# One layer of a hybrid decoder: the score matmuls of head pairs, and four waiting times in the order's planner

## The chip, the cores and the metric

The kernel runs as one program on one core of a Trainium2 chip. Its time is the device time of that core in microseconds (us); lower is better. Three runs of the kernel before gave 2163.1, 2163.2 and 2168.06 us, the median is 2163.2 us. One more execution was profiled; all views of the trace come from that one.

Engines are named as in the profile: PE is TensorE's matmuls and PEld its weight loads, DVE is VectorE, ACT is ScalarE, POOL is GpSimd, SP is SyncE, which issues every DMA of this kernel ("SPq").

## The reference, cut to what matters

```
h = rmsnorm(x);  proj = h @ w_in                        # 2048 prompt rows and 32 sample rows
qa, ka, va, ga, qb, kb, vb, gb, ma, mb = split(proj)
q, k = per-head RMS norm (gain, and 1/8 for q), head_dim 64
branch A: 8 query heads, 2 kv heads, window 128, a learned sink per head
branch B: 3 groups of 8 heads, (window, dilation) = (128,1), (512,4), (2048,16)
   # positions fall into residue classes; a block of 128 queries sees its own block of keys and the one before
   s = q @ k.T ;  s += relative position bias ;  p = exp(s - max) ;  o = p @ v / sum(p)
   # group outputs are merged with weights from max and sum
ya = (o_a * silu(ga)) @ w_up_a ;  yb = (o_b * silu(gb)) @ w_up_b
y = x + (sigmoid(ma) * ya + sigmoid(mb) * yb) @ w_out
```

The sample rows do the same against caches of past keys. New keys (after the norm and gain) and values are outputs too.

## The kernel before

**Precision.** Every large matmul is done in f16 with operands split in two: `hi` is the rounded value, `lo` the rest. A projection is three matmuls per 128 rows of contraction (hi·hi, hi·lo, lo·hi), each with a 128x128 stationary operand from the normalised input `hT` and 512 columns of weights moving. For the scores a head's 64 values of `hi` and 64 of `lo` lie under each other on the 128 partitions, for q and for k. `t.KT[0]` holds k as (hi, lo), and `t.KT[1]` a copy with the halves exchanged, (lo, hi). So two full matmuls per head give all four products: q against `KT[0]` is hi·hi + lo·lo, q against `KT[1]` is hi·lo + lo·hi, summed in the same place of the PSUM bank.

**Stages.** First come the sigmoid gates (to about 400 us). Then branch B's groups 3, 2 and 1 (to about 766, 1113 and 1436 us), each 16 tiles of 128 queries; then branch A, 16 more tiles (to about 1850 us); then up-projections and the output projection. In the 64 tiles of attention, a tile is a chain of projections q, k, v (in A: q, kv and two gates), each into one of five shared PSUM banks, 24 matmuls of 512 columns each, and a process `attend`. 22 of the 64 tiles see one block of keys, 42 see two.

**A tile's keys.** `k_chain` copies the projection out of PSUM (L730), `norm` takes squares, sums, the power of minus a half on POOL and multiplies (L738 to L751), `parts` splits into hi and lo (L303, L308), `k_turn` sends the result through a transposing DMA (L167) into `KT[0]` and then makes `KT[1]` by two DVE copies, L773, of 64 partitions each. The keys of a tile have one such place (two slots, one for even and one for odd tiles), so `k_turn` is told to wait until the tile before has been scored.

**Scores.** `attend` starts a tile's `unit`s: with two blocks of keys four units of two heads (four matmuls of 256 columns), with one block two units of four heads (eight matmuls of 128). Unit after unit takes bank 3 or bank 4 in turn (`bank[3 + y]`, lock `S_l[y]`) and fills its 512 columns. DVE reads the bank (L801: adds the bias, takes the row maximum; one instruction a head, and its accumulator read), ACT takes exponentials (L815), the result is split, transposed by DMA, and multiplied with v into bank 7 (matmuls of 64 columns).

**What sets the order.** Nothing is reordered by a compiler. The kernel is written as processes over a clock of its own (`Clock`): each instruction is appended to its engine's queue when the process reaches it, and the process then sleeps until the planner's estimate of its end (`use`, `move`, `LAT`). The clock advances by the nominal cost of each matmul. So a time in a `yield` decides only how many instructions of other processes are appended ahead, on every engine's queue; the waits between engines are semaphores that are put in by the framework from the tiles and banks that instructions touch. A matmul of a tile's first unit that finds its keys missing holds up everything behind it on PE's queue, projections of other tiles included.

**Helpers.** All matmuls are recorded at L259 and transposes on PE at L263. `load_bias` (L901) fetches the gains and biases of a group at its start. `to_pairs` (L1333) scales a finished output of branch A and transposes it on PE.

Of the kernel before, what the change touches and what calls it, by code (L numbers as in the profile page):

```python
# [150 lines left out]
def hybrid_kernel(ctx, tc, xp, xs, ca, cb1, cb2, cb3, rel_bias, norm_gain, w_in, qga, kga, sinks, qgb, kgb,  # L151
# [245 lines left out]
    def set_scale(b, am):  # L397
# [19 lines left out]
        if b.gained:  # L417
            V.tensor_scalar(b.c, b.pw, 2.0 ** -24, None, op0=OP.mult)
            V.tensor_tensor(b.tmp, b.s, b.s, op=OP.mult)
            V.tensor_scalar(b.epsc, b.tmp, EPS * 2.0 ** 20, None, op0=OP.mult)  # L420
            V.tensor_scalar(b.cu, b.c, 2.0 ** 6, None, op0=OP.mult)
            V.tensor_scalar(b.ch, b.c, 0.5, None, op0=OP.mult)
            V.tensor_scalar(b.vs, b.s, 2.0 ** -10, None, op0=OP.mult)
            yield use("V", 400)
# [256 lines left out]

    QT = [cv(8, P, dt=F16) for _ in range(2)]
    A_K = cv.off
    KTa = [cv(2, 2, P, dt=F16) for _ in range(2)]
# [41 lines left out]
    def norm(src, p0, n, nh, blk, scr, dst, gains=None, raw=None):  # L726
# [14 lines left out]
        V.tensor_scalar(st[:, 1, :nh], st[:, 0, :nh], 1.0 / 64, blk.epsc[p0:p0 + n], op0=OP.mult, op1=OP.add)  # L741
# [12 lines left out]
    def parts(dst, src, nh, scale, perm=False):  # L754

        x = heads(src)
        o = dst[:, :nh * 64].bitcast(F16).rearrange("p (h a d) -> p h a d", a=2, d=64)
        hi, lo = o[:, :, 0], o[:, :, 1]
        if perm:
            x = x.rearrange("p (j u) d -> p u j d", j=2)  # L760
            hi, lo = (v.rearrange("p (u j) d -> p u j d", j=2) for v in (hi, lo))
        yield from split(hi, lo, x, scale, nh * 64)

    def turn(dst, src, nh):

        SP.turn(dst, src[:, :nh * 64].bitcast(F16))
        yield ck.come

    def k_turn(nh, dst, cur):
        x, y = (v[:, :, cur] for v in dst)  # L770
        yield from turn(x, kn, nh)
        for j in range(2):
            V.tensor_copy(y[64 - 64 * j:128 - 64 * j], x[64 * j:64 * j + 64])  # L773
            e = use("V", 33 * nh + 65)
        yield e

    def unit(t, y, n3, us, last):
# [8 lines left out]
        for a, (x, u, j) in enumerate(hs):  # L786
            for p_ in range(2):
                ks = t.KT[p_][:, x if g else j]
                ks = ks.rearrange("p s t -> p (s t)") if nk == 2 else ks[:, cur]
                mm(bank[3 + y][:, a * w:(a + 1) * w], t.QT[:, x], ks, p_ == 0, p_ == 1, cost(w))  # L790
# [4 lines left out]
        for a, (x, u, j) in enumerate(hs):  # L795
            h = t.head(u, j)
            o, i_, b_ = sb[:, a * w:(a + 1) * w], bank[3 + y][:, a * w:(a + 1) * w], bias[:, h, (2 - nk) * P:]
# [11 lines left out]
        S_l[y].put()  # L809
# [91 lines left out]
    def load_bias(g, last):  # L901

        SP.dma_start(GR[:, g % 2], dram(GRd, 64 * g, [[0, P], [1, 64]]))
        SP.dma_start(gk_row[:, g % 2], dram(kga[0] if g == 0 else kgb[0, g - 1], 0, [[0, P], [1, 64]]))

# [51 lines left out]
    def b_tile(g, t, tok, rows, nk, cur, last, par):  # L957
# [25 lines left out]
        def k_chain(b):  # L983
            yield from stK_l.get()
            yield from norm(b.ap[:, :], 0, P, 8, blocks[f"k{g}"], kn, stK, raw=(b.lock, kn_l))
            yield from parts(kn, stK, 8, 2.0 ** 11)
# [52 lines left out]
    KT.append(cv(8, 2, P, dt=F16))  # L1039
# [16 lines left out]
    def sample_proj(g, box):  # L1056
# [20 lines left out]
        def k_chain():  # L1077
            k = sx[32:64, :kw]
            yield from norm(b.ap[32:64, :kw], 32, NS, nh, blocks[names[1]], d["sk"][1], k)
            V.tensor_tensor(heads(k), heads(k), gk_row[32:64, g % 2:g % 2 + 1].to_broadcast([NS, nh, 64]), op=OP.mult)  # L1080
            yield use("V", tv(kw))
            SP.dma_start(Ks[g][:, :], k)
            SP.dma_start(new_s[g][0].rearrange("n t a h d -> (n t) a (h d)")[:, 0], k)
# [249 lines left out]
    def to_pairs(n, o, t0, fcol):  # L1333
# [8 lines left out]
        yield ck.now + 200  # L1342
# [11 lines left out]
    def a_tile(i, t, par):  # L1354
# [52 lines left out]
        def k_chain(b):  # L1407
# [6 lines left out]
            yield from norm(k, 0, P, 2, blocks["kv0"], kn, k)  # L1414
# [4 lines left out]
            yield from parts(kn, k, 2, 2.0 ** 11)  # L1419
# [427 lines left out]
```

## Time and profile before

| | |
|---|---|
| median of three runs | 2163.2 us |
| the profiled execution's own time | 2170.46 us |
| its span, first to last instruction | 2168.6 us |
| PE busy in the span | 2029.2 us, 94% |
| DVE / ACT / POOL busy | 1386.0 / 1053.3 / 707.9 us |
| mean granted TensorE clock | 0.979 |

The profiled execution is 7.3 us above the median of the runs. The busy share of PE is that of matmuls that overlap in their pipeline, so a stretch of PE time is better read from the starts of successive matmuls. A wait of an engine is the idle time just before an instruction, put down to what ended it.

### The profile page before, as it was taken

The numbers are of one execution on the slowest core, as the hardware profiler recorded it, in microseconds if no ns is written. First come the engines' busy times: TensorE is split into PE (matmuls) and PEld (weight loads), VectorE is DVE, ScalarE is ACT, GpSimd is POOL, SyncE is SP. The second block draws the span as 40 slices with busy tenths as digits, with TensorE's granted clock in tenths as the row PEclk, the third lists the DMA queues.
The fourth block names the chain that finished last, engine by engine and source line by source line (L and its number), as shares of the span: only waits on it lengthen the run. The fifth ranks groups of instructions, "written<-read, shape, count | busy, mean of one in ns | idle before, by whom it ended". The sixth has DMA issues, their size and how long they took to land.

```text
span 2168.6 us, 36145 instructions
## 1 busy us (share of the span) xinstructions
PE 2029.2 (94%) x13042; PEld 1135.8 (52%) x13042; DVE 1386.0 (64%) x3305; ACT 1053.3 (49%) x2526; POOL 707.9 (33%) x530
## 2 busy tenths in 40 slices
PE   6999999999999899898999999997899997999999
PEld 3555555666665455554544554544455555444464
DVE  5546662576754577773767885869788898642331
ACT  5432312555555667665776766765456555300000
POOL 1000000255632245541324552426655653220110
PEclk9999999999999999999999999999999998999999
DMA  7896571368879568978857878744434366332322
GB/s 225 175 300 230 203 269 57 115 175 201 217 174 264 139 134 203 215 157 228 218 113 151 168 167 160 172 102 107 79 82 108 96 176 175 110 107 88 115 85 93
DMA packets 528389, 344.34 MB, mean 159 GB/s; under 512 B 397585, under 2 KB 427762, under 8 KB 528210
## 3 DMA queue, kind: packets, MB, share of 16 engines
q1 hardware_dynamic: 528210, 342.04, 61.4%
q8 instruction: 102, 1.67, 0.3%
q14 instruction: 77, 0.63, 0.1%
HBM read 193.53 MB, written 62.43 MB: 118 GB/s over the span
## 4 chain that ended last, share of the span: by engine, by line
PE 59%; DVE 15%; DMA 12%; ACT 5%; issue 4%; SPq 2%; POOL 2%; DVEq 0%; POOLq 0%; ACTq 0%
PE bank L259 58%; DMA arena<-arena 7%; DVE arena L308 3%; DVE arena L773 2%; DMA out_dram<-arena 2%; DVE slot L473 2%; DVE arena L801 2%; ACT arena L815 2%; SPq L161 1%; SPq L167 1%; ACT slot L470 1%; DMA hT<-arena 1%; ACT arena L303 1%; DVE arena L751 1%; POOL nst L743 1%
## 5 line engine op out<-in xcount | busy, mean ns | idle before, releaser
L259 PE MATMUL bank<-slot,hT 128*128 128x512 f16 (+1 forms) x4992 | 1127.6, 377 | 8.0 <-ACT arena L730 4.5
L259 PEld LDWEIGHTS <-hT 128*128 128x128 f16 x4992 | 546.8, 113 | 436.5 <-issue 45.2
L259 PE MATMUL bank<-hT,slot 128*128 128x416 f16 (+4 forms) x2928 | 530.8, 342 | 17.7 <-DVE slot L473 3.8
L743 POOL TENSOR_TENSOR nst<-nst,nhalf 128x8 f32<-128x8 f32 (+2 forms) x136 | 232.4, 1710 | 773.9 <-DVE nst L741 704.6
L259 PEld LDWEIGHTS <-slot 128*128 128x128 f16 x2928 | 287.2, 99 | 251.1 <-DVE slot L473 11.1
L259 PEld LDWEIGHTS <-arena 128*128 128x128 f16 x4336 | 267.9, 99 | 283.1 <-issue 88.9
L259 PE MATMUL bank<-arena 128*128 128x64 f16 (+5 forms) x3746 | 269.9, 230 | 88.6 <-DVE arena L773 44.5
L815 ACT ACTIVATE arena<-arena,ast,inv 128x256 f32<-128x256 f32 (+1 forms) x512 | 283.8, 555 | 7.0
L308 DVE SCALAR_TENSOR_TENSOR arena<-arena 128x512 f16<-128x512 f32 (+1 forms) x292 | 221.6, 772 | 92.2 <-ACT arena L303 91.2
L303 ACT ACTIVATE arena<-arena 128x512 f16<-128x512 f32 (+2 forms) x395 | 231.3, 607 | 98.6 <-DMA arena<-arena 53.8
L1172 POOL TENSOR_TENSOR arena<-arena 128x512 f32<-128x512 f32 (+1 forms) x102 | 140.1, 1373 | 120.7 <-DVE arena L1215 101.4
L259 PE MATMUL bank<-slot,arena 128*128 128x512 f16 x768 | 167.9, 379 | 2.1 <-DVE slot L473 1.6
L473 DVE SCALAR_TENSOR_TENSOR slot<-slot,gsc 128x512 f16<-128x512 f32 (+1 forms) x144 | 107.3, 745 | 86.7 <-ACT slot L470 86.2
L730 ACT ACTIVATE arena<-bank 128x512 f32<-128x512 f32 x112 | 65.8, 589 | 173.4 <-PE bank L259 89.4
L643 ACT ACTIVATE arena<-bank,wst 128x416 f32<-128x416 f32 (+2 forms) x82 | 48.7, 597 | 190.5 <-PE bank L259 162.9
L470 ACT ACTIVATE slot<-slot,gsc 128x512 f16<-128x512 f32 (+1 forms) x144 | 98.1, 681 | 73.2 <-DVE slot L473 63.7
L303 ACT ACTIVATE arena<-arena,yk 128x512 f16<-128x512 f32 (+2 forms) x40 | 25.5, 638 | 201.1 <-POOL arena L1706 186.4
L1706 POOL TENSOR_TENSOR arena<-arena 128x512 f32<-128x512 f32 (+2 forms) x40 | 48.7, 1218 | 221.2 <-DVE arena L1692 201.7
L801 DVE CUSTOM_DVE_ANT_0 arena<-bank,bias 128x128 f32<-128x128 f32 (+1 forms) x296 | 87.4, 343 | 50.2 <-PE bank L259 48.9
L740 DVE TENSOR_REDUCE nst<-arena 128x8 f32<-128x512 f32 (+2 forms) x136 | 85.6, 630 | 42.3 <-ACT arena L738 41.6
L773 DVE COPY arena<-arena 64x1024 f16<-64x1024 f16 (+1 forms) x128 | 77.5, 605 | 54.0 <-DMA arena<-arena 52.3
L810 ACT ACTIVATE ast<-ast,ninv 128x2 f32<-128x2 f32 (+1 forms) x212 | 61.2, 289 | 102.6 <-DVE ast L801 101.7
(167 smaller groups left out, 1758.5 us busy)
## 6 DMA issues: line engine op xcount, KB each, us to landing
arena<-in_cache_b_kv_dram SPq DMA_DIRECT2D x144, 256.0 KB
slot<-in_w_in_dram SPq DMA_DIRECT2D x64, 512.0 KB
arena<-Qs SPq DMA_DIRECT2D x96, 256.0 KB
arena<-in_w_in_dram SPq DMA_DIRECT2D x16, 1024.0 KB
gates<-arena SPq DMA_DIRECT2D x78, 208.0 KB
comb<-arena SPq DMA_DIRECT2D x48, 264.0 KB
arena<-comb SPq DMA_DIRECT2D x48, 264.0 KB
arena<-gates SPq DMA_DIRECT2D x24, 512.0 KB
```

The lines of the kernel that those rows point to most:

```text
L259: T.matmul(out, l, r, start=start, stop=stop)
L303: A.activation(hi, src, AF.Copy, scale=scale)
L308: V.scalar_tensor_tensor(lo, src, scale, hi, op0=OP.mult, op1=OP.subtract)
L470: A.activation(b.part(0, k), src, AF.Copy, scale=sc)
L473: V.scalar_tensor_tensor(b.part(1, k), src, sc, b.part(0, k), op0=OP.mult, op1=OP.subtract)
L730: A.activation(dst, src, AF.Copy)
L740: V.tensor_reduce(st[:, 0, :nh], heads(s), axis=AX.X, op=OP.add)
L743: G.tensor_tensor(st[:, 2, :nh], st[:, 1, :nh], nhalf[p0:p0 + n].to_broadcast([n, nh]), op=OP.pow)
L773: V.tensor_copy(y[64 - 64 * j:128 - 64 * j], x[64 * j:64 * j + 64])
L801: V.tensor_tensor_reduce(out=o, in0=i_, in1=b_, scale=1.0, scalar=-3e38 if g else sinkS[:, u, j:j + 1], op0=OP.add, op1=OP.max, accum_out= ...
L815: A.activation(e, e, AF.Exp, bias=nm[:, x:x + 1], scale=inv[:, g:g + 1], accum_out=l[:, x:x + 1])
L1172: G.tensor_tensor(sprod[:n], q, k, op=OP.mult)
```

## The change

It has two parts.

**The scores.** The layout of q and k within a pair of heads (j = 0, 1) changes: q of head 0 lies as (hi, lo), q of head 1 as (lo, hi); k of head 0 as (lo, hi), k of head 1 as (hi, lo). One full matmul per head now gives the two cross products. `KT[1]` holds only the hi of k, in the 64 partitions where q's hi of that head lies, and a second matmul over these 64 partitions gives hi·hi; lo·lo is no longer computed. The second matmuls of a pair stand in different halves of the array's rows and write to different banks: head 0 to bank 3, head 1 to bank 4. So each unit now writes both banks, and the two units that share them take columns 0 to 255 and 256 to 511 (`place`). The copies behind the turn move half as many values. The factor of 2^11 on k moves from the split into the norm (so that the split has the scale 1.0 and its second step is a plain subtraction), and the gains in `gk_row` are scaled by 2^-11 by one added DVE instruction in `load_bias`, directly behind the DMA that brings them.

**Margins.** Four estimates of the planner grow: behind a turn of q or k by 1500 ns; between the reading of a score bank and its being free for the next unit by 500 ns; in `to_pairs` from 200 to 900 ns.

```
-            V.tensor_scalar(b.ch, b.c, 0.5, None, op0=OP.mult)
+            if b.name[0] == "k":
+                V.tensor_scalar(b.ch, b.epsc, 2.0 ** -22, None, op0=OP.mult)
+            else:
+                V.tensor_scalar(b.ch, b.c, 0.5, None, op0=OP.mult)
...
-    KTa = [cv(2, 2, P, dt=F16) for _ in range(2)]
+    KTa = [cv(2, 2, P, dt=F16), cv(1, 2, P, dt=F16)]
...
-        V.tensor_scalar(st[:, 1, :nh], st[:, 0, :nh], 1.0 / 64, blk.epsc[p0:p0 + n], op0=OP.mult, op1=OP.add)
+        V.tensor_scalar(st[:, 1, :nh], st[:, 0, :nh], 2.0 ** -28 if key else 1.0 / 64, (blk.ch if key else blk.epsc)[p0:p0 + n],
+                        op0=OP.mult, op1=OP.add)
...
-    def parts(dst, src, nh, scale, perm=False):
+    def parts(dst, src, nh, scale, perm=False, key=False):
-        x = heads(src)
-        o = dst[:, :nh * 64].bitcast(F16).rearrange("p (h a d) -> p h a d", a=2, d=64)
-        hi, lo = o[:, :, 0], o[:, :, 1]
-        if perm:
-            x = x.rearrange("p (j u) d -> p u j d", j=2)
-            hi, lo = (v.rearrange("p (u j) d -> p u j d", j=2) for v in (hi, lo))
+        x = heads(src).rearrange("p (j u) d -> p u j d" if perm else "p (u j) d -> p u j d", j=2)
+        o = dst[:, :nh * 64].bitcast(F16)
+        first, then = (bass.AP(tensor=o.tensor, offset=o.offset + c, ap=[o.ap[0], [256, nh // 2], [w, 2], [1, 64]])
+                       for c, w in ((0, 192), (64, 64)))
+        hi, lo = (then, first) if key else (first, then)
         yield from split(hi, lo, x, scale, nh * 64)

     def turn(dst, src, nh):
         SP.turn(dst, src[:, :nh * 64].bitcast(F16))
-        yield ck.come
+        yield ck.come + 1500

     def k_turn(nh, dst, cur):
         x, y = (v[:, :, cur] for v in dst)
         yield from turn(x, kn, nh)
         for j in range(2):
-            V.tensor_copy(y[64 - 64 * j:128 - 64 * j], x[64 * j:64 * j + 64])
-            e = use("V", 33 * nh + 65)
+            V.tensor_copy(y[64 * j:64 * j + 64], x[64 - 64 * j:128 - 64 * j, j::2])
+            e = use("V", 17 * nh + 65)
         yield e

     def unit(t, y, n3, us, last):
...
-        for a, (x, u, j) in enumerate(hs):
-            for p_ in range(2):
-                ks = t.KT[p_][:, x if g else j]
-                ks = ks.rearrange("p s t -> p (s t)") if nk == 2 else ks[:, cur]
-                mm(bank[3 + y][:, a * w:(a + 1) * w], t.QT[:, x], ks, p_ == 0, p_ == 1, cost(w))
+        def place(a, j):
+            o = 256 * y + a // 2 * w
+            return bank[3 + j][:, o:o + w]
+
+        def keys(v):
+            return v.rearrange("p s t -> p (s t)") if nk == 2 else v[:, cur]
+
+        for v in range(0, len(hs), 2):
+            for a, (x, u, j) in enumerate(hs[v:v + 2], v):
+                mm(place(a, j), t.QT[:, x], keys(t.KT[0][:, x if g else j]), True, False, cost(w))
+            for a, (x, u, j) in enumerate(hs[v:v + 2], v):
+                r = slice(64 * j, 64 * j + 64)
+                mm(place(a, j), t.QT[r, x], keys(t.KT[1][r, u if g else 0]), False, True, cost(w) / 2)
...
-            o, i_, b_ = sb[:, a * w:(a + 1) * w], bank[3 + y][:, a * w:(a + 1) * w], bias[:, h, (2 - nk) * P:]
+            o, i_, b_ = sb[:, a * w:(a + 1) * w], place(a, j), bias[:, h, (2 - nk) * P:]
...
-        S_l[y].put()
+        ck.at(ck.now + 500, S_l[y].put)
...
     def load_bias(g, last):
         SP.dma_start(gk_row[:, g % 2], dram(kga[0] if g == 0 else kgb[0, g - 1], 0, [[0, P], [1, 64]]))
+        V.tensor_scalar(gk_row[:, g % 2], gk_row[:, g % 2], 2.0 ** -11, None, op0=OP.mult)
...
-            yield from norm(b.ap[:, :], 0, P, 8, blocks[f"k{g}"], kn, stK, raw=(b.lock, kn_l))
-            yield from parts(kn, stK, 8, 2.0 ** 11)
+            yield from norm(b.ap[:, :], 0, P, 8, blocks[f"k{g}"], kn, stK, raw=(b.lock, kn_l), key=True)
+            yield from parts(kn, stK, 8, 1.0, key=True)
...
     def to_pairs(n, o, t0, fcol):
-        yield ck.now + 200
+        yield ck.now + 900
```

What this makes of the program is seen in the order of instructions. On PE, in the middle of group 1 (its ninth tile, two blocks of keys), the rows of the kernel before are these. `arena` holds q, k and the transposed probabilities, `slot` the weights of the projections, `hT` the normalised input; in brackets stand the semaphores waited for, DMAHW those of DMAs and DVE that of VectorE:

```order
L259 LDWEIGHTS arena_95 [waits DMAHW7_49]
L259 MATMUL bank3_99<-arena_95 128x256 [waits DMAHW4_49]
L259 LDWEIGHTS arena_95
L259 MATMUL bank3_99<-arena_95 128x256 [waits DVE_49]
...
L259 MATMUL bank6_102<-slot0_67,hT0_65 128x512
...
L259 LDWEIGHTS arena_95
L259 MATMUL bank4_100<-arena_95 128x256
```

The tile's first unit fills bank 3 and waits for the turn and for the copies L773; nine projection matmuls later the second unit fills bank 4 and waits for nothing. The same place of the changed program:

```order
L259 LDWEIGHTS arena_95 [waits DMAHW6_49,DMAHW7_49]
L259 MATMUL bank3_99<-arena_95 128x256 [waits DVE_49]
L259 LDWEIGHTS arena_95
L259 MATMUL bank4_100<-arena_95 128x256 [waits DVE_49]
L259 LDWEIGHTS arena_95
L259 MATMUL bank3_99<-arena_95 128x256 [waits DVE_49]
L259 LDWEIGHTS arena_95
L259 MATMUL bank4_100<-arena_95 128x256 [waits DVE_49]
...
L259 MATMUL bank2_98<-slot0_67,hT0_65 128x512
...
L259 MATMUL bank3_99<-arena_95 128x256 [waits DVE_49]
```

Each unit now alternates between the banks, and its first matmul on each bank waits for DVE: the value that it waits for is that of the accumulator read behind the last instruction with which DVE reads this bank for the unit just before, though that one used the other half of the columns. Before, the value was that of the unit before the last. Between the first and the second unit stand six projection matmuls here, where there were nine. Over the program, the first matmul of 156 of the 212 units carries such a wait for the unit directly before it. The number of matmuls is unchanged (12931 in the program), and 512 of the 1024 score matmuls now use 64 rows of the array. Changes of the array's tile shape from one matmul to the next were 76 and are now 581.

In the same program the projections between a tile's k projection and its first score matmul grow: 75 matmuls of 512 columns in the ninth tile of group 3 become 93, 72 in the ninth tile of group 1 become 150.

On DVE, at the start of group 2, the added scaling of the gains stands between work of the running tiles:

```order
L756 TENSOR_TENSOR arena<-arena,nst 128x512
L476 SCALAR_TENSOR_TENSOR slot_68<-slot_68,gsc 128x512
L308 SCALAR_TENSOR_TENSOR arena<-arena 128x512
L919 TENSOR_SCALAR gk_row<-gk_row 128x64
L744 TENSOR_REDUCE nst<-arena 128x8
L745 TENSOR_SCALAR nst<-nst,wst 128x8
```

Row L919 is new, and it waits for the DMA that is issued at the same point of the program.

More of the change, by code (lines that the diff above doesn't have):

```diff
@@ L724, in hybrid_kernel, with norm @@
     start.biased = 4
-    def norm(src, p0, n, nh, blk, scr, dst, gains=None, raw=None):
+    def norm(src, p0, n, nh, blk, scr, dst, gains=None, raw=None, key=False):
         if raw:
@@ L1038, in hybrid_kernel @@
     cv = Carve(sampB["end"])
-    KT.append(cv(8, 2, P, dt=F16))
+    KT.append(cv(4, 2, P, dt=F16))
     QT.append(cv(8, P, dt=F16))
@@ L1079, in k_chain @@
             yield from norm(b.ap[32:64, :kw], 32, NS, nh, blocks[names[1]], d["sk"][1], k)
-            V.tensor_tensor(heads(k), heads(k), gk_row[32:64, g % 2:g % 2 + 1].to_broadcast([NS, nh, 64]), op=OP.mult)
+            V.scalar_tensor_tensor(heads(k), heads(k), 2.0 ** 11, gk_row[32:64, g % 2:g % 2 + 1].to_broadcast([NS, nh, 64]),
+                                   op0=OP.mult, op1=OP.mult)
             yield use("V", tv(kw))
@@ L1413, in k_chain @@
             k = kv[:, :128]
-            yield from norm(k, 0, P, 2, blocks["kv0"], kn, k)
+            yield from norm(k, 0, P, 2, blocks["kv0"], kn, k, key=True)
             if last:
@@ L1418, in k_chain @@
                 SP.dma_start(npa[0, 0].rearrange("t a h d -> t a (h d)")[:, 0], kn[:, 384:])
-            yield from parts(kn, k, 2, 2.0 ** 11)
+            yield from parts(kn, k, 2, 1.0, key=True)
             yield from cond(ck, lambda: prev.scored and (i > 1 or last_b.valued))
```

## The prediction

> **What bounds the kernel now.** I read the page first, then the stages, then PE's waits there.
>
> ```profile
> span 2168.6 us, 36145 instructions
> PEclk9999999999999999999999999999999998999999
> PE 59%; DVE 15%; DMA 12%; ACT 5%; issue 4%; SPq 2%; POOL 2%; DVEq 0%; POOLq 0%; ACTq 0%
> 400.00:766.00 366.00, 340.53 (x2111) 214.62 (x2110) 229.54 (x609) 213.28 (x540) 161.78 (x107) 0.97 0.70 180
> 766.00:1113.00 347.00, 319.73 (x2225) 173.90 (x2224) 239.96 (x584) 230.60 (x574) 133.78 (x89) 0.98 0.81 189
> 1113.00:1436.00 323.00, 308.25 (x2224) 161.03 (x2224) 241.71 (x562) 219.77 (x539) 132.69 (x92) 0.98 0.75 157
> 1436.00:1850.00 414.00, 372.95 (x2829) 224.64 (x2828) 357.05 (x921) 226.89 (x617) 224.53 (x185) 0.96 0.48 117
> ```
>
> The last four rows are group 3, group 2, group 1 and branch A; their columns are the stretch, then busy us of PE, PEld, DVE, ACT and POOL, then granted clock and DMA. PE leads the chain with 59% and is busy in 90 to 95% of these stages, so its work counts almost in full, and so does what it waits for. DVE is next, at 63 to 86%. PE's waits, in these 1450 us:
>
> ```profile
> PE bank L259 <- DVE arena L773: 44.5, 32, 4.7
> PE bank L259 <- DMA arena<-arena: 27.8, 20, 6.5
> PE bank L259 <- DVE ast L801: 12.6, 7, 4.0
> PE bank L263 <- DVE arena L1340: 7.4, 6, 2.4
> PE bank L259 <- ACT arena L730: 4.5, 1, 4.5
> ```
>
> (us in all, times, longest.) The first is the wait of scores for the exchanged keys, the third for a score bank; of the second only 4.2 us stand before scores (3.2 and 1.0 in the rows of the next fence), the rest before the products with v, which the change leaves alone. The clock of 0.96 to 0.98 costs 0.03·366 + 0.02·347 + 0.02·323 + 0.04·414 = 41 us at most.
>
> **PE's work, first what it saves.** The rows of a score matmul:
>
> ```profile
> L259 PE MATMUL bank<-arena 128*128 128x256 f16 x672 | 106.8, 277 | 36.4 <-DVE arena L773 22.2 <-DVE ast L801 12.6 <-DMA arena<-arena 1.0
> L259 PE MATMUL bank<-arena 128*128 128x128 f16 x352 | 30.2, 226 | 25.6 <-DVE arena L773 22.3 <-DMA arena<-arena 3.2
> 1004.66 0.55 PE L259 MATMUL bank<-arena 128*128 128x128 f16 x7 [0.77 <-DVE arena L773]
> 1005.05 0.81 PE L259 MATMUL bank<-slot,hT 128*128 128x512 f16 x3
> 766.73 5.36 PE L891 MATMUL bank<-slot,hT 128*32 128x512 f16 x72
> 772.02 1.27 PE L259 MATMUL bank<-slot,hT 128*128 128x512 f16 x5
> ```
>
> 672 is 16 in each of 42 tiles, 352 is 16 in each of 22. Seven of 128 columns take 1005.05 − 1004.66 = 0.39 us, 0.056 each; of 256 columns four take 0.43 (1256.98 to 1257.41, below), 0.108 each. No matmul on half the rows is in this trace. The nearest are the sample projections in three column strips: 72 matmuls in 5.29 us are 24 threes at 0.22, against 0.217 for one of full width, so neighbours in one tiling ran together. I take that for row halves too. The second pass of a pair then costs one matmul and some 4 ns instead of two: 168 pairs save 0.104 us each and 88 pairs 0.052, together 22.1 us. If they don't overlap it is 0.
>
> **PE's work, what it costs.** A change of the tile shape isn't free:
>
> ```profile
> 1486.82 2.11 PE L259 MATMUL bank<-slot,hT 128*128 128x512 f16 x9
> 1488.86 0.44 PE L263 MATMUL bank<-ident,arena 32*128 32x32 f32 x4
> 1455.46 0.61 PE L259 MATMUL bank<-arena 128*128 128x256 f16 x4
> 1456.01 0.83 PE L891 MATMUL bank<-slot,hT 128*32 128x512 f16 x12
> ```
>
> Nine matmuls at 0.217 are 1.95, and the transposes on 32 rows start after 2.04: 0.09 us more. Four of 256 columns are 0.43, and the strips start after 0.55: 0.12, of which a part belongs to the change before. Leaving the strips at 772.02 took 5.29 − 24·0.217 = 0.08. So some 0.094 us a change, by rows or by columns, whatever ran before. The order has 581 changes for 76: 505·0.094 = 47.5 us more, on PE's own path. PE's work grows by 47.5 − 22.1 = 25.4 us, if 64 rows pay what 32 do; from the 32-row case I see no reason against it.
> The Trainium skill, "TensorEngine Tiling (Array Packing)", section Tiling Modes, says that a change of the mode drains TensorE while a change of the tile within it does not; it gives no figure, and the sum by it is this one.
>
> **What the margins take away.** The first scores of a tile move behind more projections (75 to 93 and 72 to 150 in the two tiles counted), 18 of them 3.9 us; the longest wait for L773 was 4.7. Copies of half the values help by another half of 0.55:
>
> ```profile
> L773 DVE COPY arena<-arena 64x1024 f16<-64x1024 f16 x96 | 53.2, 554 | 41.9 <-DMA arena<-arena 40.6
> L773 DVE COPY arena<-arena 64x256 f16<-64x256 f16 x32 | 24.3, 759 | 12.1 <-DMA arena<-arena 11.7
> DVE arena L773 <- DMA arena<-arena: 52.3, 34, 4.6
> ```
>
> So I take 44 of the 44.5 us and the 4.2 of the turns as gone; with the margin of 1.5 us alone about two thirds would go (the waits with 1.5 us taken off each leave a third), which is the low end, 30. L1340: 0.7 us off each of six waits is 4 of 7.4. The 12.6 for L801 go, but into the next term.
>
> **The wait that comes in their place.** Both units of a pair now lie in the same banks, and the order shows the wait for the reading of the unit just before. Whether it is late is read from before: a tile of group 1.
>
> ```profile
> 1251.63 0.49 PE L259 MATMUL bank<-arena 128*128 128x256 f16 x3 [0.62 <-DVE arena L773]
> 1252.89 0.08 DVE L801 DVE_READ_ACCUMULATOR2_ANT ast<- 128x1 f32 x1
> ...
> 1256.98 0.60 PE L259 MATMUL bank<-arena 128*128 128x256 f16 x4
> 1257.41 2.11 PE L259 MATMUL bank<-slot,hT 128*128 128x512 f16 x9
> 1259.36 0.60 PE L259 MATMUL bank<-arena 128*128 128x256 f16 x4
> 1257.26 1.28 DVE L306 TENSOR_TENSOR arena<-arena 128x512 f16<-128x512 f32 x2
> 1259.66 1.75 DVE L751 TENSOR_TENSOR arena<-arena,nst 128x512 f32<-128x512 f32 x1
> 1261.34 0.41 DVE L801 CUSTOM_DVE_ANT_1 arena<-bank,bias 128x256 f32<-128x256 f32 x1
> 1261.68 0.08 DVE L801 DVE_READ_ACCUMULATOR2_ANT ast<- 128x1 f32 x1
> 1250.70:1264.60 13.90, 13.28 (x91) 7.10 (x90) 13.78 (x32) 9.93 (x24) 9.05 (x7) 1.00 0.79 173
> L801 DVE DVE_READ_ACCUMULATOR2_ANT ast<- x512: 71/83/89, 419.5 to 1834.9; 128x1 f32 x171
> ```
>
> The third unit's matmuls are those of 1256.98, the fourth's start at 1259.36. DVE, busy 13.78 of 13.90 us in this burst with other tiles' splits and norms as well, reads the third's first head only at 1261.34 to 1261.76. Under the new rule the fourth unit would wait 2.4 us, and behind it stand the projections of the next tile, which nothing else holds up. I did the same for all 64 tiles, with the starts of the 1024 score matmuls and the ends of the 512 accumulator reads (last row: first and last). Taking the latest boundary of each tile, since one wait moves the rest, gives 99.9 us: 5.6 in the 22 tiles of one block, 94.3 in the 42 of two. Adding every boundary instead gives 132.8. Against it: DVE loses half of 77.5 us of copies, and a PE that has waited hands it work later. In its favour: fewer projections between units (nine to six above). The low end is 10, where DVE reads at once: the first unit's last matmul starts at 1251.85, and its read ends at 1252.97, 1.1 us later and less than the 2 us to the next unit. The upper end is 157, were the new order's gaps laid against the old reads. I take three quarters of 99.9, 75 us: DVE's copies are a small part of the work between reads.
> The Trainium skill, "PSUM — Partial Sum Buffer", section on bank collisions, asks for semaphores by bank and quadrant and not by address, since another address in the bank collides too. By it half a bank is no buffer of its own; the waits in the order agree with that. No run here shows a collision.
>
> **Small terms.** The scaling of `gk_row` makes DVE wait for a DMA four times. The nearest rows are L773's waits for DMA, 52.3 us in 34 (the row above), 1.5 each, 6 in all. Behind the waiting instruction stand sums of norms and splits, for which q and k of the next tiles wait, and through them PE; it loses 0 to 18 (four times the longest 4.6 on DVE), I take 4. Keys that are scored later hold the buffer of the next k, and so its bank before L730; PE waited for that once, 4.5 us, with five banks to take from. I take 0, up to 10. The k split as a plain subtraction, the new places of hi and lo, the scaled norm and the sample's extra factor keep counts and sizes: 0, within DVE's gaps; uncovered, some tens of ns each. The clock I leave: waits go and waits come; ±20.
>
> **Sum.** +47.5 − 22.1 − 44 − 4.2 − 4 − 12.6 + 75 + 4 = +39.6 us. The profiled execution's 2170.5 us becomes 2210; from the median of 2163.2 it is **2203 us**.
>
> **Rivals.**
> *The margins win (not slower).* One mechanism: DVE keeps up, because scores come when it is less loaded, so the bank's reading is over before the next unit. It decides where the new wait falls under 75 − 39.6 = 35 us. At 10 us, and half the clock's 41 us regained with the waits, it is 2163.2 + 39.6 − 65 − 20 = 2118. For it: in group 3 all 16 boundaries were early by 1 us or more, and the copies halve. Against: DVE's 357 of 414 us in branch A, and lateness in 33 of the 42 tiles of two blocks.
> *The wait is worse:* all of the 157, 2203 + 82 = 2285. For it: the gaps shrink. Against: waits that overlap.
> *Row halves don't run together:* +22.1, 2225. No row speaks to it directly; the strips speak against.
> *Row halves change without a drain:* −47.5, 2155.5. Against it the 32-row transposes.
>
> **How the numbers follow.** The forecast 0.55, own range 2175 to 2245 (wait of 47 to 117); the margins win 0.28; worse wait 0.07; no overlap 0.05; no drain 0.05. The range of 2125 to 2255 leaves out most of the worse wait and a third of the margins' case. What a measurement can tell from no change is about 0.3%, 6.5 us: faster 0.29, same 0.06, slower 0.65.
>
> **What would show it.** In the profile after: no wait of scores for the copies over 10 us in all (if 30 or more, the margins are too small); a wait of score matmuls for DVE's reading (L815 there) of 50 to 110 us, mostly in groups 2, 1 and branch A; group 3 shorter by some 10 us, as it has no late reading; before a 64-row matmul and behind it about 0.09 us more than without; two 64-row matmuls starting within 10 ns. The forecast is wrong if that wait is under 35 us.

## The result and the profile after

The changed kernel takes 2223.7 us (median of four runs, 2215.5 to 2229.0), the kernel before 2163.4 beside it: a ratio of 1.027, 95% interval 1.023 to 1.031. It is slower, by 60 us; 2203 was forecast. The profiled execution took 2226.0 us, against 2170.5 before, so 55.5 us of loss can be looked at in the trace.

From the page after and from its table of stages (columns as before: the stretch, busy us of PE, PEld, DVE, ACT and POOL, granted clock). The stretches are set so that they begin at the same tiles as those of before, which lasted 366, 347, 323 and 414 us:

```profile
span 2224.0 us, 36102 instructions
PE 65%; DVE 13%; DMA 9%; ACT 4%; issue 4%; SPq 2%; POOL 2%; ACTq 0%; POOLq 0%; DVEq 0%
400.00:781.00 381.00, 354.86 (x2146) 214.91 (x2147) 229.02 (x601) 211.66 (x536) 156.78 (x107) 0.97 0.67 173
781.00:1150.00 369.00, 343.13 (x2313) 171.31 (x2308) 247.45 (x603) 234.44 (x582) 140.85 (x94) 0.96 0.78 180
1150.00:1461.00 311.00, 299.60 (x2120) 145.61 (x2119) 227.41 (x555) 215.93 (x535) 130.38 (x90) 0.99 0.75 160
1461.00:1893.00 432.00, 379.49 (x2788) 211.00 (x2787) 366.65 (x915) 226.42 (x618) 226.70 (x179) 0.94 0.44 108
```

PE's share of the chain rose from 59 to 65%: more of the end is set by PE's own work. Groups 3 and 2 and branch A grew by 15, 22 and 18 us, group 1 shrank by 12. (PE moves other stages' projections between them, so a stage's time tells where work was done, and the whole tells what it cost. The rest of the loss, 13 us, lies behind branch A, where PE has 35 matmuls more than before.)

PE's waits after (us in all, times, longest):

```profile
PE bank L259 <- DVE arena L779: 27.7, 14, 5.6
PE bank L259 <- ACT arena L734: 21.8, 6, 7.0
PE bank L259 <- DVE ast L815: 21.6, 17, 4.8
PE bank L259 <- DMA arena<-arena: 13.1, 14, 2.4
...
PE bank L263 <- DVE arena L1356: 4.3, 1, 4.3
...
PE bank L259 <- ACT arena L1014: 4.0, 1, 4.0
```

L779 is the copies (L773 before), L734 ACT's emptying of a bank of k or q (L730), L815 the reading of the scores (L801), L1356 the scaled output (L1340), L1014 ACT's emptying of a bank of v (L999). The wait for the copies should have gone and is 27.7; the new wait in the shared banks should have been 75 and is 21.6; and PE stands 21.8 us at L734, at banks that ACT has not emptied, against 4.5 before.

The new score matmuls, in PE's timeline: a unit of group 1 (two full matmuls of 256 columns, then two on 64 rows), and a tile of group 3 (two such pairs of 128 columns):

```profile
1214.63 0.59 PE L259 MATMUL bank<-slot,hT 128*128 128x512 f16 x2
1215.07 0.60 PE L259 MATMUL bank<-arena 128*128 128x256 f16 x4
1215.59 6.65 PE L259 MATMUL bank<-slot,hT 128*128 128x512 f16 x30
518.57 0.81 PE L259 MATMUL bank<-slot,hT 128*128 128x512 f16 x3
519.22 0.82 PE L259 MATMUL bank<-arena 128*128 128x128 f16 x8
519.97 0.87 PE L259 MATMUL bank<-slot,hT 128*128 128x512 f16 x3
```

The unit takes 1215.59 − 1215.07 = 0.52 us where four full ones took 0.43, and the eight of 128 columns 0.75 us where they took 0.45. From the starts of all 1024: a 64-row matmul starts 205 ns after the full one before it (median of 162, without one in between 109), the two halves start 3 ns apart (163 pairs), and the next full one starts 212 ns after the second (102). So in this trace a change of the tile shape costs 96 ns on the way in and 103 on the way out; with 128 columns it is 96 and 103 again (152 and 159 against 56).

Adding up the distances between the starts of the 13042 matmuls of the trace, the 55.5 us are: shape changes +48.1, slower matmuls right behind one +4.6, halves that run together −21.2, gaps (PE's waits over 0.15 us between matmuls) +6.9, lower clock +12.7, the rest +4.4.

### The profile page after: what moved, and what is told of

Its sections match the earlier page's. It is cut to its first block, busy times and chain, and to the rows that moved or that the text cites. A ratio compares the mean times of both kernels' runs of the same rounds, so it can differ in the third digit from the quotient of the medians.

```text
span 2224.0 us, 36102 instructions
## 1 busy us (share of the span) xinstructions
PE 2074.5 (93%) x13042; PEld 1109.0 (50%) x13042; DVE 1390.9 (63%) x3309; ACT 1051.4 (47%) x2526; POOL 716.2 (32%) x530
## 4 chain that ended last, share of the span: by engine, by line
PE 65%; DVE 13%; DMA 9%; ACT 4%; issue 4%; SPq 2%; POOL 2%; ACTq 0%; POOLq 0%; DVEq 0%
PE bank L259 63%; DMA out_dram<-arena 3%; DMA arena<-arena 3%; DVE arena L308 2%; DVE arena L815 2%; DVE slot L476 1%; ACT arena L829 1%; SPq L167 1%; SPq L161 1%; ACT arena L303 1%; DMA hT<-arena 1%; PE bank L905 1%; POOL arena L1188 1%; DVE arena L306 1%; POOL nst L748 1%
## 5 line engine op out<-in xcount | busy, mean ns | idle before, releaser
L259 PE MATMUL bank<-slot,hT 128*128 128x512 f16 (+1 forms) x4992 | 1136.6, 379 | 29.9 <-ACT arena L734 21.8
L259 PEld LDWEIGHTS <-hT 128*128 128x128 f16 x4992 | 539.2, 114 | 489.7 <-issue 82.8
L259 PEld LDWEIGHTS <-arena 128*128 128x128 f16 x4336 | 245.8, 98 | 302.3 <-issue 113.7
L259 PE MATMUL bank<-arena 128*128 128x64 f16 (+8 forms) x3746 | 279.9, 232 | 70.3 <-DVE arena L779 27.7
L308 DVE SCALAR_TENSOR_TENSOR arena<-arena 128x512 f16<-128x512 f32 (+1 forms) x228 | 191.0, 841 | 92.1 <-ACT arena L303 91.8
L1188 POOL TENSOR_TENSOR arena<-arena 128x512 f32<-128x512 f32 (+1 forms) x102 | 140.8, 1381 | 142.7 <-DVE arena L1231 110.0
L306 DVE TENSOR_TENSOR arena<-arena 128x512 f16<-128x512 f32 (+2 forms) x167 | 130.8, 790 | 52.2 <-ACT arena L303 51.5
L815 DVE CUSTOM_DVE_ANT_0 arena<-bank,bias 128x128 f32<-128x128 f32 (+1 forms) x296 | 87.6, 343 | 56.3 <-PE bank L259 55.2
L734 ACT ACTIVATE arena<-bank 128x512 f32<-128x512 f32 x112 | 65.7, 589 | 111.0 <-DMA out_dram<-arena 67.4
```

Of the source, the lines that this page charges most:

```text
L259: T.matmul(out, l, r, start=start, stop=stop)
L306: V.tensor_tensor(lo, src, hi, op=OP.subtract)
L308: V.scalar_tensor_tensor(lo, src, scale, hi, op0=OP.mult, op1=OP.subtract)
L734: A.activation(dst, src, AF.Copy)
L815: V.tensor_tensor_reduce(out=o, in0=i_, in1=b_, scale=1.0, scalar=-3e38 if g else sinkS[:, u, j:j + 1], op0=OP.add, op1=OP.max, accum_out= ...
L1188: G.tensor_tensor(sprod[:n], q, k, op=OP.mult)
```

## The experiments

They were run on three chips, where the kernel before had medians of 2174.8 to 2175.8 us, and not 2163.4 as beside the changed kernel. So each is compared by its ratio to the kernel before on its own chip, with the 95% interval in brackets; on that scale 0.0046 is 10 us, and "us slower" is worked out from the ratio. The changed kernel was not run again there: its 1.027 (1.023 to 1.031) is that of its own chip, and a difference to it is known to some 10 us only. The first four expectations are in us of the chip where the kernel before takes 2163.

**The margins alone** (three lines; that of the turn counts for q and for k). The kernel before with

```diff
-        yield ck.come
+        yield ck.come + 1500
-        S_l[y].put()
+        ck.at(ck.now + 500, S_l[y].put)
-        yield ck.now + 200
+        yield ck.now + 900
```

> The kernel before with the three planned margins alone (1.5 us behind a turn, 0.5 us before a score bank is free, 0.9 us behind the scaled output); scores, copies and norms as before. Theory of the tile shapes (the change loses by its matmuls on 64 rows, not by its margins): scores wait less for the copies (44.5 us before, about 15 left), for the bank (12.6, about 5 left) and for the turns, no tile shape is added, so 2163 - 30 - 8 - 8 = some 2117 to 2140. Rival (the margins only put scores behind other work, and their buffers come free later): 2155 to 2175, with new waits of PE for banks that ACT or DVE empty.

Measured: 2206.0 us, 1.0143 (1.0118 to 1.0169), 31 us slower than before, with not one instruction added. PE's waits:

```profile
PE bank L259 <- DMA arena<-arena: 39.9, 26, 6.0
PE bank L259 <- DVE arena L773: 38.9, 22, 5.2
PE bank L259 <- ACT arena L999: 14.3, 4, 5.8
PE bank L259 <- ACT arena L730: 12.3, 8, 7.2
...
PE bank L259 <- DVE ast L801: 3.6, 2, 2.7
```

Against the rows of before, the wait for the copies barely fell (44.5 to 38.9) and the one for the score bank did (12.6 to 3.6), but PE stands 12 us more at L999, 8 more at L730 and 12 more at transfers. On the scale of the expectation the time is 2194 us. The expectation failed, and so did its rival, which ended at 2175; the new waits for banks that ACT empties are the rival's.

**The scores alone.** The changed kernel with these three lines as before.

> The changed kernel with the three margins undone, so the new scores alone. Theory of the tile shapes: PE's work grows by 48 us of shape changes and 5 of slow matmuls behind them, less 21 of halves that run together, +32; the waits for the copies stay near 40 instead of 28, and the wait for the reading in the shared banks, without its margin, is 40 to 80 instead of 22: 2240 to 2290. Rival (the margins carry the loss): at most 2200.

Measured: 2216.4 us, 1.0186 (1.0159 to 1.0213), 41 us slower than before.

```profile
PE bank L259 <- DVE arena L779: 29.3, 19, 5.8
...
PE bank L259 <- DVE ast L815: 22.4, 19, 4.5
```

On the scale of the expectation this is 2204 us: neither the 2240 to 2290 of the theory nor the rival's "at most 2200". The two waits are smaller than the theory had them. That for the copies goes from 44.5 to 29.3 without any margin, and the wait in the shared banks is 22.4 without the margin of 0.5 us, as with it. That the halved copies do this is not shown: the next two runs have them too, one with 32.1 and one with 48.7, and the score bank's margin alone on the kernel before, with whole copies, has 33.8. PE's work grew much as in the changed kernel (shape changes +49.6, behind them +4.7, halves −21.4: 33 us of the 41). Margins and scores together lose less (59 us on this scale) than one by one (31 + 41).

**The second pass on all rows.** The changed kernel with

```diff
-            for a, (x, u, j) in enumerate(hs[v:v + 2], v):
-                r = slice(64 * j, 64 * j + 64)
-                mm(place(a, j), t.QT[r, x], keys(t.KT[1][r, u if g else 0]), False, True, cost(w) / 2)
+                mm(place(a, j), t.QT[:, x], keys(t.KT[1][:, u if g else 0]), False, True, cost(w) / 2)
```

> The changed kernel with the second pass of every head on all 128 rows instead of 64, each right behind its first pass: no tile shape is added, and no halves run together. It adds the low keys' products of the other head to the scores, so what the softmax gets is not the reference's. The places in the banks, the waits and the order of the rest are as in the changed kernel. Theory of the tile shapes: -48 - 5 + 21 = -32, so 2192 (2183 to 2200); by a drain that only uses time in which PE would wait anyway 2210 to 2224; if the shapes cost nothing in the end, 2224 + 21 = 2245.

(What is added is the low part of the queries with the other head's high keys.) Measured: 2211.2 us, 1.0165 (1.0137 to 1.0192). That is 0.0105 or 23 us less than the changed kernel; 32 were expected, and on that scale the 2199 us lie just within the 2183 to 2200. PE's own work is 33 us less in the trace, as the theory of the tile shapes has it, but its waits grew by 20.6 us (154.2 against 133.6 in gaps). Time that PE spends on changes of the shape hides some of the waits for others, so only a part of this work counts: about two thirds by the ratios, 12 of 33 us by the two traces.

**The same with a bank for each unit.** Beside that run's edit,

```diff
         def place(a, j):
-            o = 256 * y + a // 2 * w
-            return bank[3 + j][:, o:o + w]
+            return bank[3 + y][:, a * w:(a + 1) * w]
```

> As the run with the second pass on all rows, with one bank for each unit as in the kernel before (the two heads of a unit side by side in it) instead of both units in halves of both banks. Again the scores are not the reference's. Theory that the shared banks cost the waits that the profile puts down to them: 21.6 us less than that run, about 2170. Rival (PE, once past that wait, stands at the next one, for copies or for banks): 5 to 12 us less, 2180 to 2187. The wait as I forecast it (75 us): 2117.

Measured: 2212.8 us, 1.0158 (1.0118 to 1.0199): no gain over the shared banks. All three forecasts failed; from the two intervals a gain of more than some 10 us is excluded, a smaller one is not. The waits with shared banks, then with a bank for each unit:

```profile
PE bank L259 <- DVE arena L779: 32.1, 19, 5.9
PE bank L259 <- DMA arena<-arena: 26.5, 18, 4.7
PE bank L259 <- DVE ast L813: 26.4, 19, 4.8
```

```profile
PE bank L259 <- DVE arena L779: 48.7, 23, 7.8
PE bank L259 <- DMA arena<-arena: 31.1, 24, 3.6
PE bank L259 <- ACT arena L734: 23.8, 7, 7.4
```

The 26.4 us for the reading (L813 here) are gone, and PE stands 16.6 us more at the copies, 4.6 at transfers and 4.3 at L734 instead. The order of the engines is the same in both, so this also tests how I had sized the term. Measured in the run with own banks as I had measured it in the kernel before, where no wait depends on the reading, DVE is late by 113 us (the latest boundary of each tile, summed). With the dependence, in the same order, it makes PE wait for 26.4. A reading of this that no run tests: the readings lag behind a PE that runs ahead, and once PE is held up, there or for the copies, DVE catches up.

**Each margin alone**, on the kernel before; first the turn's.

> The kernel before with the margin of 1.5 us behind a turn alone. All three margins together cost 31 us (1.4%), where I had expected a gain. Theory that the turn's margin carries it (tiles start later in the plan, more projections are put ahead of them, and these stand at banks that ACT has not emptied): 20 to 35 us slower than before, waits for the copies near 40 us, and those for ACT's emptying of banks (4.5 and 2.2 us in the kernel before) at 20 to 30 together. Rival (each margin costs a third): about 10 us slower.

Measured: 2190.1 us, 1.0076 (1.0052 to 1.010), 16.5 us slower. This margin carries the largest part, though it is under the 20 to 35 that were expected; the waits are near what was expected (33.4 for the copies, 27.8 at banks that ACT empties).

> The kernel before with the margin of 0.5 us before a score bank is free alone. Theory of the turn's margin: within 8 us of before; the wait for the score bank (12.6 us) falls to about 5. Rival (each margin costs a third): 10 us slower. If the order is what decides, and any new order loses, 15 or more slower.

Measured: 2172.5 us, 0.9976 (0.9957 to 0.9996), 5 us faster, with the wait for the score bank at 5.1, as expected: the one version with all its outputs that is faster than the kernel before, if only by 0.2%.

> The kernel before with the 0.9 us instead of 0.2 behind the scaled output alone. Theory of the turn's margin: within 6 us of before; the wait for these outputs (7.4 us in six) falls to about 4. Rival (each margin costs a third): 10 us slower.

Measured: 2181.4 us, 1.0029 (1.0011 to 1.0047), 6 us slower; the wait for this output all but went (7.4 to 0.9), and others grew by more (transfers 27.8 to 37.5, L730 4.5 to 8.0). The three sum to some 18 us, and together they cost 31: the margins act on one order and don't add.

What the turn's margin does on ACT and PE. ACT's waits for stores and PE's waits that answer to them, before:

```profile
ACT arena L730 <- DMA out_dram<-arena: 80.1, 13, 10.6
ACT arena L999 <- DMA out_dram<-arena: 24.0, 7, 10.3
PE bank L259 <- ACT arena L999: 2.2, 1, 2.2
```

and with the turn's margin alone:

```profile
ACT arena L730 <- DMA out_dram<-arena: 105.5, 16, 8.9
ACT arena L999 <- DMA out_dram<-arena: 49.3, 12, 7.8
PE bank L259 <- DVE arena L773: 33.4, 20, 5.7
PE bank L259 <- ACT arena L730: 16.0, 6, 7.6
PE bank L259 <- ACT arena L999: 11.8, 3, 5.2
```

ACT empties a bank of k or v into a staging buffer (`stK`, `stV`). From there the tiles whose rows are kept write them out, and the plan counts the buffer as free when this store is issued, not when it has landed. The next emptying stands at the store, the bank stays full, and PE stands at the bank. The margin brings 51 us more of this to ACT. All of PE's waits for ACT, added up, go from 14 to 41 us. Those at banks of L730 and L999 go from 6.7 to 28.9, and before 27.6 of the 28.9 the instruction of ACT that PE waits for has itself just stood at a store.

**The stores left out**, once without and once with the turn's margin. (They are 42 of 256 KB by the trace's DMA table, where the expectations counted 45; and of the 14.3 us of PE's waits for ACT only 6.7 are at banks of L730 and L999.)

```diff
-            SP.dma_start(rows[:, :512], stK)
+            ck.move(rows[:, :512])
-                SP.dma_start(rows[:, 512:], stV)
+                ck.move(rows[:, 512:])
```

> The kernel before without the 45 stores of the tiles' new rows of k and v from their staging buffers; those outputs stay unwritten, and the order of the engines is the same. In the kernel before ACT's copies that empty the banks of k and v stand 104 us behind these stores, and PE stands 14.3 us at banks that ACT empties. Theory of the staging buffers: 5 to 15 us faster than the kernel before. Rival (ACT's standing is covered): within 3 us.

> The kernel before with the turn's margin of 1.5 us, and without the same 45 stores (those outputs unwritten; the order as in the run with the turn's margin alone). Theory of the staging buffers: the 16 us that the margin costs are PE's 26 us more at banks that ACT empties, behind copies that stand at the stores (155 us instead of 104); so without the stores the margin costs at most 5 us or gains, beside the run of the kernel before without them, and is 20 to 35 us faster than with them. Rival (the margin costs by putting scores later): it stays 12 to 20 us slower than the kernel before without stores.

Measured: 2136.2 us, 0.9831 (0.9798 to 0.9864) without the margin; 2115.6 us, 0.9725 (0.9702 to 0.9749) with it. The margin that costs 16.5 us with the stores gains 21 without them (by the medians; 23 by the ratios), and with the margin the stores cost 76 us, where 20 to 35 were expected. PE's waits, first without the margin (no wait for L730 is left), then with it:

```profile
PE bank L259 <- DVE arena L773: 32.8, 33, 3.2
```

```profile
PE bank L259 <- DVE arena L773: 14.8, 15, 2.8
...
PE bank L259 <- ACT arena L730: 0.9, 2, 0.7
```

Here the margin does what it was forecast to do: half of the wait for the copies goes. Without the stores the kernel before gains 37 us, far more than the 14 that PE shows as waits for ACT and more than I had expected (5 to 15). In the traces PE's gaps fall by 22 us (12 of them at the copies, 7 at ACT, 4.5 at the score bank) and the loss by the lower clock by 10. PE's waits for transfers do not fall (27.8 and 29.8), which speaks against the stores' traffic as the cause. From the first score of group 3 to that of group 2, where 16 tiles in a row are kept, it takes 343.9 us before and 367.4 with the margin; without the stores 324.9 and 315.1.

**Half passes apart.** The changed kernel with

```diff
                 mm(place(a, j), t.QT[:, x], keys(t.KT[0][:, x if g else j]), True, False, cost(w))
-            for a, (x, u, j) in enumerate(hs[v:v + 2], v):
                 r = slice(64 * j, 64 * j + 64)
```

> The changed kernel with each head's second pass right behind its first, in the same order otherwise: the two halves of a pair do not run together, and each pair has four changes of the tile shape instead of two. PE's own work grows by 256 x 2 x 0.10 = 51 us of changes and 168 x 0.106 + 88 x 0.053 = 22 of halves that stood together, 73 in all. The run with all rows lost 33 us of PE's work against the changed kernel and 13 to 23 us of time, so about a half of such work is taken from waits: 73 gives 35 to 55 us more than the changed kernel, a ratio to before of 1.043 to 1.053. Rival (all of it counts, the waits stay): 1.06. Rival (the waits of DVE's chain set the pace, PE's work is free): below 1.035.

Measured: 2262.4 us, 1.0409 (1.0369 to 1.0449), 30 us above the changed kernel, a little under the 35 to 55 expected. A tile of group 3:

```profile
522.15 0.81 PE L259 MATMUL bank<-slot,hT 128*128 128x512 f16 x3
522.79 1.34 PE L259 MATMUL bank<-arena 128*128 128x128 f16 x8
524.07 0.87 PE L259 MATMUL bank<-slot,hT 128*128 128x512 f16 x3
```

1.28 us for the eight, against 0.75 with the halves together. Over the whole trace PE's work grew by 75 us (shape changes 102.3 against 49.5, a count that also takes in changes at which PE waited and so lies a little above the 48.1, and 22.5 of halves that had stood together), while its gaps fell from 133.6 to 114.4. So 30 of 75 us counted here, and 23 of 33 in the run on all rows.

**The scaling of the gain row.** In the changed kernel's timeline, the third of its four times, and PE's next wait:

```profile
1075.46 0.20 DVE L919 TENSOR_SCALAR gk_row<-gk_row 128x64 f32<-128x64 f32 x1 [12.28 <-DMA gk_row<-in_k_gain_b_dram]
1075.58 0.42 DVE L815 CUSTOM_DVE_ANT_0 arena<-bank,bias 128x256 f32<-128x256 f32 x1
1076.39 0.30 ACT L824 ACTIVATE ast<-ast,ninv 128x2 f32<-128x2 f32 x1 [10.99 <-DVE ast L815]
...
1079.14 4.00 PE L259 MATMUL bank<-slot,hT 128*128 128x512 f16 x9 [6.58 <-ACT arena L734]
```

DVE stands 12.3 us at a small transfer, with the reading of scores queued behind it; ACT stands 11.0 us for that reading, with a bank's emptying behind it; PE stands 6.6 us at the bank. The run takes L919 away:

```diff
-        V.tensor_scalar(gk_row[:, g % 2], gk_row[:, g % 2], 2.0 ** -11, None, op0=OP.mult)
```

> The changed kernel without DVE's scaling of the gain row; the new rows of k that are written out are too large by 2^11, and the order of the other instructions is the same. In the changed kernel DVE stands 6.1, 12.3 and 6.5 us at this instruction, and PE 7.0, 6.6 and 2.2 us right behind. Theory: 10 to 16 us faster than the changed kernel, a ratio to before of 1.020 to 1.023. As I forecast the term (4 us): 1.025. Rival (PE meets its next wait instead): 1.027.

Measured: 2221.4 us, 1.0228 (1.0187 to 1.0268), 0.0042 or 9 us below the changed kernel. The two intervals overlap, so the 9 us are not settled; the rival (1.027) lies just outside the interval. Of the three waits that the theory counts, 6.6 and 2.2 us are gone. The 7.0 us are not: in the changed kernel they stand behind ACT at a store,

```profile
729.33 0.60 ACT L734 ACTIVATE arena<-bank 128x512 f32<-128x512 f32 x1 [5.03 <-DMA out_dram<-arena]
729.97 3.83 PE L259 MATMUL bank<-slot,hT 128*128 128x512 f16 x9 [7.04 <-ACT arena L734]
```

and the same matmul waits as long without the scaling:

```profile
726.22 0.60 ACT L734 ACTIVATE arena<-bank 128x512 f32<-128x512 f32 x1 [10.98 <-DMA out_dram<-arena]
726.87 4.00 PE L259 MATMUL bank<-slot,hT 128*128 128x512 f16 x9 [6.76 <-ACT arena L734]
```

So 8.8 us of PE's waits hang on the scaling, not 15.8. All of PE's waits together did not fall (140.8 to 143.7), and the loss by the lower clock is 9 us less, so what the scaling costs in time stays open.

**A plan that knows of the stores.** The kernel before with the margins for the turn and the score bank, and

```diff
             SP.dma_start(rows[:, :512], stK)
+            yield ck.come + 2000
             stK_l.put()
...
                 SP.dma_start(rows[:, 512:], stV)
-            stV_l.put()
+                ck.at(ck.come + 2000, stV_l.put)
+            else:
+                stV_l.put()
```

> The kernel before with the margins behind the turn and before the score bank (not the one behind the outputs), and with a plan that knows of the stores: the staging buffers of k and v count as free 2 us after the planned landing of their store, not when it is issued. All is computed and written. Theory of the staging buffers: PE is no longer sent to banks whose copies stand at a store, so its 41 us at banks that ACT empties (turn's margin alone) fall under 20 us, and the time under that of the turn's margin alone (2190) by 15 to 35 us: 2155 to 2175, as fast as the kernel before (2175) or faster. Rival (the plan puts whole tiles off and runs short of other work, as it did with the turn's margin): 2180 or more, with the waits for the copies or the transfers grown instead.

Measured: 2178.8 us, 1.0018 (1.0005 to 1.0032): 13 us faster than the turn's margin alone, of which the score bank's margin may be 5 (it gains that by itself), but 4 us slower than before, between the 2175 of the theory and the 2180 of the rival. ACT, then PE:

```profile
ACT arena L730 <- DMA out_dram<-arena: 14.7, 4, 5.1
PE bank L259 <- DVE arena L773: 16.6, 19, 2.8
PE bank L259 <- ACT arena L730: 15.2, 12, 3.6
PE bank L259 <- ACT arena L1000: 8.5, 7, 2.5
```

ACT's 155 us behind stores fell to 20 (15 of them at L730), and the wait for the copies to 16.6, near the 14.8 without stores. But PE's waits for ACT did not fall (43 us in all, 25 of them at L730 and L1000). They are now many and short (12 times 1.3 us at L730) instead of few and long, and only one of them, 3.6 us, stands right behind a store: PE still meets banks that ACT has not emptied, for some other reason. What that is stays open. So does the way in which the stores cost their 37 us, since with ACT's standing nearly gone, and the stores still there, the time is not better than before.

## Why the prediction was right, and where only its total was

The direction and the size came out (2223.7 in a range of 2175 to 2245, +60 where +40 was forecast), and the price of PE's own work was right. The wait that was to make up the loss was not, and that the total is near is luck, as the terms show.

**The shape changes (+47.5): right.** +48.1 in the trace, at 96 and 103 ns each where 94 had been read off matmuls on 32 rows and 32 columns. Missing was the matmul behind the way back, 10 to 11 ns slower in the median and 19 in the mean: +4.6. The runs on all rows and with halves apart confirm the term from both sides, and add that only some 0.4 to 0.7 of such work reaches the time, since PE waits less when it works longer. The Trainium skill, "TensorEngine Tiling (Array Packing)", section Tiling Modes, says that a change of the mode drains TensorE; the trace agrees that it takes time, 96 and 103 ns. **The halves (−22.1): right**, −21.2, with 3 ns between their starts. With these, PE's work grew by 31.5 us where the forecast had 25.4.

**The margins and copies (−44): wrong.** The wait for the copies went from 44.5 to 27.7. By the signs named, that is nearly the 30 at which the margins would be too small. The step that failed is "the first scores of a tile move behind more projections", which took the rest of the pipeline as given. The later scores also let PE run on to banks that ACT had not yet emptied, because ACT stood at stores. With the stores out of the kernel before, the turn's margin takes away 18 of 32.8 us and gains 21. With them it costs 16.5. In the changed kernel's own trace, followed back from each wait by what released what, 18.7 of the 27.7 us at the copies have a store within the 25 us before. No run took the stores out of the changed kernel; and that ACT's standing is the way in which they cost is argued, since the plan that nearly removed it left the time where it was before.

**The bank before L730 (0, up to 10): wrong, and in part the same mechanism.** +17.3 there, +23.5 over all of PE's waits for ACT (14.3 to 37.8). I had looked at who holds the buffer of the *next* k until it is scored; what holds it in the two waits of before is the staging buffer's store, which stood in that trace with 104 us on ACT. I passed over it since PE showed only 6.7 us for L730 and L999. In the changed kernel, of 27.7 us at L734 and L1014 the store explains less than half: 11.1 us (7.04 and 4.03) are right behind ACT at a store, 6.6 behind the gain row, and at the other 10.0 ACT was late with other work, 6.3 of them in branch A. ACT's standing at stores is the same 119 us there with the margins and without, while PE's waits for ACT are 37.8 and 20.2.

**The shared banks (+75): mis-sized.** 21.6 us in the profile, and nothing that can be measured in the time: with own banks the run on all rows took as long. The lateness of the readings was read rightly (113 us in the same order where nothing depends on them); that three quarters of it would become PE's wait was wrong. By the point that I had named, 35 us, the forecast's mechanism failed and the margins should have won. They did not: the margins, which were to gain, cost time themselves (31 us on the kernel before), and waits at L734 and at the copies stood where the forecast had none. The Trainium skill, "PSUM — Partial Sum Buffer", section on bank collisions, asks for semaphores by bank and quadrant and not by address; the order's waits agree.

**The gain row (+4): too small.** Two waits of PE behind it, 6.6 + 2.2 = 8.8 us, go with it; what that is in time is not settled (9 us, with intervals that overlap). I had priced it by waits on DVE for transfers of another kind, the longest 4.6; once the tiles ran it waited 6.1, 12.3 and 6.5.

**The other terms.** L1340: 7.4 to 4.3, forecast −4. Scores on turns: 4.2 to about 1, as forecast; the products with v waited 12 us less for transfers too, which the forecast had left alone. The clock, taken as 0, cost 12.7 us. It varied by as much among the other runs (some 22 us lost without stores and with the margin, 39.8 before), and no run was made for it. Group 3 should have been 10 us shorter and is 11 longer, 22 longer with the margins alone (from its first score to that of group 2).

So all of PE's waits grew by 6.6 us (134.2 to 140.8) where the forecast had +14.2, out of parts of −65 and +79 that were both far too large. The total was near because PE's own work was right, and two wrong parts offset each other. Taken out of the changed kernel one by one, the 64-row matmuls are worth 23 us, the margins 18 and the scaling perhaps 9, of 59; whether they add was not tested.

## What to carry to other kernels

Matmuls on fewer rows lose if only a pair of them stands between full ones: two changes of the shape cost 0.2 us, about twice what a 256-column matmul takes, and two halves run together save one. Before an order is changed so that PE runs further ahead, look for what holds the engine that empties its banks, even where PE shows little of it: here 42 stores, with 104 us of ACT behind them, turned a margin worth 21 us into a loss of 16. And lateness measured where nothing waits is no forecast of a wait: 113 us of it became 26, and removing those gained nothing that could be measured. Before a wait is put down to the thing in front of it, see whether it goes when that thing is taken out: 7.0 us beside the gain row stayed.

## What the runs showed of the hardware that was not expected

The price of a change of the tile shape is the same for 128 and 256 columns (96 ns in and 103 out), and within some 10 ns the same whether rows or columns change: by the starts in the trace before, 93 to 94 ns into the strips or into 32 rows, and 95 to 96 out of the strips. The first matmul after the return to full rows is slower too, whatever its columns (66 for 56, 120 for 109, 227 for 216 ns in the median of 44, 24 and 137). And without the 42 stores, 11 of 344 MB that move, a kernel whose PE is busy for 94% of the span gains 37 us, well over twice what the profile shows as PE's waits for ACT, the engine that stands at them; the gaps of all PE's waits fell by 22 us without them, and the loss by the lower clock by 10 (39.8 to some 30).
